# A hybrid decoder layer: projections by plain and by seven block products, block sums spread out, wider elementwise operations

## The chip, the cores and the metric

The kernel runs on one core of a Trainium2 chip. The metric is device time in microseconds (us). A core has a matrix engine (PE, with its weight loads listed apart as PEld), a vector engine (DVE), an activation engine (ACT), GpSimd (POOL) and a queue engine (SP) that issues most DMAs.

## What is computed

A decoder layer on x of 2048 tokens by 1024 features, all in float32. One projection feeds two mixers: a gated short convolution and a causal attention over three dilated windows. Their outputs are normalised, projected back, and a SwiGLU feed-forward follows.

```python
h = rms_norm(x, g_mix)
u, gb, gc, q, k, v = split(h @ w_in)          # six parts of 512 columns
y_conv = gb * short_conv(gc * u, conv_w)       # causal, width 3
q = rms_norm(q per head, g_q) * 64 ** -0.5     # 8 heads of 64
k = rms_norm(k per head, g_k)
y_attn = dilated_mixture(q, k, v)              # windows (128,1), (512,4), (2048,16)
x = x + concat(rms_norm(y_conv, g_conv_out), rms_norm(y_attn, g_attn_out)) @ w_out
h = rms_norm(x, g_ffn)
x = x + (silu(h @ w_gate) * (h @ w_up)) @ w_down
```

## The kernel before, in words

**Precision.** Each float32 operand is split into two float16 parts, hi and lo. A product is three float16 matmuls added up in PSUM (hi·hi, hi·lo, lo·hi). A split is a cast on ACT that gives hi, and a subtraction on another engine that gives lo.

**Tiles.** x is held as its transpose, in hi and lo, in four chunks c of 512 tokens; a chunk is eight tiles of 128 features by 512 tokens (`self.x[c]`). The 8 heads are taken as four pairs g.

**Stages.** The first is the norm of x with its DMA transposes, mixed with convolution block 0 (`conv_steps` with j = 0, called in `in_and_conv`): 4 chunks, and in each 3 products (gate C, u, gate B) of 24 matmuls. The second are the projections of q, k, v: 16 calls of `project(g, c, W)`, four chunks for each of four pairs; pair 3 takes the chunks backwards. The third is attention (`attention_pairs`, `attn_steps`): 160 steps, into which the rest of the convolution (blocks 1 to 3) and the half of the output projection that belongs to it (`tail_out`) are mixed as filler, `RATE` filler steps for each attention step. A filler step is three matmuls of 128x512 (`mm3_steps`, lines 191 to 193). The fourth are the other half of the output projection and the feed-forward; they aren't touched.

**Seven products of eight.** `project` multiplies a chunk of x (two token halves, two feature halves) by a pair's 384 columns (two column halves, one per head, of 192: q, k, v) by a scheme of seven block products in place of eight. It needs sums of blocks of both sides. `operands(g)` makes those of the weights: three loads, the largest element (`vmax`, a reduce of 3072 elements at L96), 8 scalings on ACT (L1163), combinations on GpSimd, and seven splits into tiles of the pool `ring` (ACT L1171, DVE L1172). `sums(c)` makes those of x, for two halves of a chunk: each takes two adds on GpSimd (L1134), four additions on DVE (L1137 to L1140), two casts on ACT (L1144) and two subtractions on DVE (L1145). Two `sums` calls stand in convolution block 0, two ahead of the first `project` calls.

**One call of `project`.** It works in two units t. A unit has three PSUM banks of 192 columns, from the pool `mm` or `cvx` in turn, and 84 matmuls (L1237). The banks are emptied into `f` while it runs: twice by ACT (L1247, L1254), five times by DVE (L1244). Then the epilogue: squares into `row` (ACT L1264), v split (ACT L1267, DVE L1268), sums of the squares (DVE L1274), a root by Ln and Exp (ACT L1275, L1276), and on GpSimd the scaling of q and k into `row` (L1285), the gain of k (L1290); then casts of `row` (ACT L1294, L1295) and subtractions (GpSimd L1296, L1297), and the stores to d_v and d_qk. There is one `row` and one `qkhl` for all calls.

**What else runs beside the projections.** `spill_conv(j, m)` splits the weights of convolution blocks 1 to 3, one third m at a time (through `weights`, ACT L149 and DVE L150, 8 of each) and writes them to DRAM for the filler. `spill_out` does so with the output weights (ACT L1333, DVE L1334). The table `SPILLS` says after which `project` call each runs.

**Order.** Each engine runs its instructions in the order in which they are written down; a scheduler that simulates the program sets that order. `tc.issue_after(x)` keeps what is emitted inside it from being placed before instruction x. Pools limit what is alive at once: `ring` has 9 tiles, `f` 3, `cvx` 4 PSUM banks.

Of the kernel before, what the change touches and what calls it, by code (L numbers as in the profile page):

```python
# [9 lines left out]
F32 = mybir.dt.float32  # L10
# [8 lines left out]
P = 128  # L19
# [7 lines left out]
HD = 64  # L27
# [983 lines left out]
class Fast(Builder):  # L1011
# [5 lines left out]
    RATE = 2.2  # L1017
# [16 lines left out]
    def in_and_conv(self):  # L1034
# [5 lines left out]
        with ExitStack() as c:  # L1040
# [11 lines left out]
            self.uc = cp.tile([P, 9], F32, name="uc")  # L1052
# [32 lines left out]
            ring = None  # L1085
            n = -1
            for step in self.conv_steps(0, W, before):
# [28 lines left out]
            self.st = dict()

    SPILLS = {(0, 3): (0,), (1, 0): (1, 2), (1, 2): (3,), (1, 3): (4,), (2, 0): (5, 6), (2, 2): (7,), (2, 3): (8,),
              (3, 0): (9, 10), (3, 1): (11, 12)}

    def sums(self, c, s0):
# [5 lines left out]
        Sc = self.sums_of[c] = [pool.tile([P, 2, 2, 4, 256], F16, name=name, bufs=2) for _ in range(2)]  # L1127
        xh, xl = self.x[c]
        for t in range(2):
            y = []  # L1130
            for i in range(2):
                o = slice((2 * t + i) * P, (2 * t + i + 1) * P)
                y.append(self.tmp.tile([P, KC, P], F32, name="t4"))
                nc.gpsimd.tensor_tensor(y[i], xh[:, :, o], xl[:, :, o], op=ALU.add)  # L1134
            a11, a12, a21, a22 = (y[i][:, 4 * k:4 * k + 4] for i in range(2) for k in range(2))
            v = nc.vector
            v.tensor_tensor(a22, a21, a22, op=ALU.add)  # L1137
            v.tensor_tensor(a21, a11, a21, op=ALU.subtract)
            v.tensor_tensor(a11, a22, a11, op=ALU.subtract)
            v.tensor_tensor(a12, a12, a11, op=ALU.subtract)  # L1140
            for i in range(2):
                src = y[i].rearrange("p (a k) t -> p a k t", a=2)
                hi, lo = (Sc[i][:, :, q, :, t * P:(t + 1) * P] for q in range(2))
                nc.scalar.copy(hi, src)  # L1144
                v.tensor_tensor(lo, src, hi, op=ALU.subtract)  # L1145

    def operands(self, g):
# [25 lines left out]
        p = nc.gpsimd  # L1173
        split(0, b11)
# [12 lines left out]
    def qk_constants(self):  # L1187
# [18 lines left out]
        self.vs = [self.fq.tile([P, 4, 2, 2, HD + 1], F16, name=f"vs{i}") for i in range(2)]  # L1206
# [4 lines left out]
    def project(self, g, c, W):  # L1211
# [8 lines left out]
        n = self.row.rearrange("p (j b d) -> p j b d", j=4, b=4)  # L1220
        F = []
        for t in range(2):
            pool, name = ((self.psmm, "mm"), (self.cvx, "cvx"))[self.units % 2]
            self.units += 1
            ps = [pool.tile([P, 512], F32, name=name)[:, 0:192] for _ in range(3)]

            def left(m, q, k):
                if m in (0, 1, 3):
                    i, k0 = {0: (2 * t, 0), 1: (2 * t, 4), 3: (2 * t + 1, 4)}[m]
                    return (xh, xl)[q][:, k0 + k, i * P:(i + 1) * P]  # L1230
                i, a = {5: (0, 0), 2: (0, 1), 6: (1, 0), 4: (1, 1)}[m]
                return Sc[i][:, a, q, k, t * P:(t + 1) * P]

            def product(m):
                for k in range(4):
                    for q, (x, y) in enumerate(((0, 0), (0, 1), (1, 0))):
                        nc.tensor.matmul(ps[self.BANK[m]], lhsT=left(m, x, k), rhs=W[m][:, y, k],  # L1237
                                         start=m in (0, 5, 4) and k == 0 and q == 0, stop=k == 3 and q == 2,
                                         skip_group_check=True)
            f = fq.tile([P, 2, 2, 192], F32, name="f", bufs=3)  # L1240
            F.append(f)

            def plus(o, bank, z):
                nc.vector.scalar_tensor_tensor(o, bank, u, z, op0=ALU.mult, op1=ALU.add)  # L1244
            f11, f12, f21, f22 = (f[:, i, h] for i in range(2) for h in range(2))
            product(0)
            nc.scalar.activation(f21, ps[0], AF.Copy, scale=u)  # L1247
            product(5)
            plus(f12, ps[1], f21)
            product(4)  # L1250
            if (g, c, t) == (0, 0, 0):
                self.squares(3, self.last, self.pstr.tile([P, 4], F32, name="tr"), False)
            product(1)
# [313 lines left out]
    def attention_pairs(self):  # L1567
# [9 lines left out]
        for _ in islice(fill, 24):  # L1577
            pass
# [315 lines left out]
```

## Time and profile before

| | us |
|---|---|
| median of 3 runs | 2207.26 (2206.59 to 2209.81) |
| the profiled execution | 2208.49 |
| its span in the trace | 2206.7 |
| PE busy | 2030.8 (92% of the span) |
| DVE busy | 1526.2 (69%) |
| ACT busy | 1047.4 (47%) |
| GpSimd busy | 726.7 (33%) |
| first matmul of the projections | at 132.71 |
| first matmul of attention (L1498) | at 473.35 |
| first matmul of the output projection's second half | at 836.92 |

Times in the trace count from the start of the span. A row of a window view gives busy time and number of instructions of each engine in a stretch, then PEclk (the clock that PE was granted, 1.00 is full), the mean busy share of the DMA engines, and GB/s. A row of the groups gives a line, its engine and operation, the tiles it writes and reads, a count, the busy time, the mean of one in ns, and the idle time ahead of them with what ended it. A row of the waits gives what was waited for, the total in us, how often, and the longest.

### The profile page before, as it was taken

To read this page: it belongs to the slowest core of one execution; us is meant where nothing else is said; L and a number is where in the kernel's file an instruction comes from. 1 tells how busy PE (TensorE), PEld (TensorE's weight loads), DVE (VectorE), ACT (ScalarE), POOL (GpSimd) and SP (SyncE) were. 2 spreads that over 40 slices of the span, in tenths; PEclk is the share of its full clock that TensorE was granted. 3 is DMA by queue.
4 is the path that set the end of the run, shared out by engine and by line. 5 is a ranking of instruction groups with operands and counts; after the bars stand their busy time and mean duration, and the time that the engine had idled before them with its cause. 6 is when DMAs were issued, how large, how long until landed. Compare 5 with 4: busy or idle time off the path is not lost.

```text
span 2206.7 us, 34303 instructions
## 1 busy us (share of the span) xinstructions
PE 2030.8 (92%) x12984; PEld 1115.8 (51%) x12984; DVE 1526.2 (69%) x2893; ACT 1047.4 (47%) x1967; POOL 726.7 (33%) x614
## 2 busy tenths in 40 slices
PE   3868778989999978998999999999999999999998
PEld 1347778946665653443444444444444444444443
DVE  7999885537776886687676666667676676545454
ACT  6445544447775766655333333334333244444341
POOL 2333434433433321122221112112222146555463
PEclk8879789999999998999999999999999999999999
DMA  9524454935867557799522332233222563251442
GB/s 240 138 84 138 158 154 130 192 74 148 180 136 193 167 140 200 244 248 293 161 101 91 101 115 82 91 107 113 90 95 102 210 243 123 77 178 53 130 139 87
DMA packets 460160, 317.00 MB, mean 144 GB/s; under 512 B 255568, under 2 KB 413264, under 8 KB 457808
## 3 DMA queue, kind: packets, MB, share of 16 engines
q1 hardware_dynamic: 442304, 291.56, 46.3%
q10 hardware_dynamic: 17680, 23.16, 2.9%
q8 instruction: 103, 1.69, 0.3%
q14 instruction: 73, 0.60, 0.1%
HBM read 157.96 MB, written 116.85 MB: 125 GB/s over the span
## 4 chain that ended last, share of the span: by engine, by line
PE 46%; issue 5%; DVE 4%; DMA 2%; SPq 2%; ACT 2%; POOL 1%; DVEq 0%; POOLq 0%; ACTq 0%
PE ps L812 28%; PE ps L945 15%; SPq L199 2%; DVE hl L680 1%; PE mm L191 1%; PE mm L192 1%; DVE w L933 1%; PE mm L193 1%; PE ps L191 1%; PE ps L192 0%; PE ps L193 0%; POOL x L952 0%; DMA b<-b 0%; ACT wq L742 0%; DMA wq<-d_a 0%
## 5 line engine op out<-in xcount | busy, mean ns | idle before, releaser
L812 PEld LDWEIGHTS <-w 128*128 128x128 f16 x3696 | 362.2, 98 | 448.0 <-issue 12.7
L812 PE MATMUL ps<-b,w 128*128 128x512 f16 x2112 | 464.8, 381 | 8.7 <-DMA b<-d_h 3.1
L945 PE MATMUL ps<-b,w 128*128 128x512 f16 x1848 | 399.7, 379 | 1.4 <-DVE s L966 0.8
L812 PE MATMUL ps<-hb,w 128*128 128x512 f16 x1584 | 347.1, 379 | 0.0
L945 PEld LDWEIGHTS <-w 128*128 128x128 f16 x1848 | 180.8, 98 | 220.1 <-issue 2.6
L705 POOL TENSOR_TENSOR t<-wq 128x512 f32<-128x512 f32 (+1 forms) x46 | 59.6, 1297 | 407.3 <-issue 231.1
L818 DVE TENSOR_TENSOR s<-ps,s 128x512 f32<-128x512 f32 x220 | 150.1, 683 | 37.1 <-PE ps L812 36.6
L952 POOL TENSOR_TENSOR x<-x,s 128x512 f32<-128x512 f32 x72 | 103.4, 1437 | 170.4 <-DVE s L966 133.1
L1511 DVE TENSOR_TENSOR et<-sm,et 128x512 f16<-128x512 f32 (+1 forms) x160 | 126.3, 807 | 41.8 <-ACT et L1510 40.8
L953 DVE SCALAR_TENSOR_TENSOR x<-ps,a_u,x 128x512 f32<-128x512 f32 x96 | 71.8, 749 | 101.7 <-PE ps L945 75.2
L1505 ACT ACTIVATE sm<-s,bound,kap 128x512 f32<-128x512 f32 (+1 forms) x160 | 116.6, 754 | 53.8 <-DVE s L1503 45.0
L191 PE MATMUL mm<-b,wq 128*128 128x512 f16 x320 | 125.7, 393 | 10.1 <-ACT cg L1360 8.6
L193 PE MATMUL mm<-b,wq 128*128 128x512 f16 x320 | 125.1, 391 | 3.4 <-DVE wq L150 3.4
L1237 PEld LDWEIGHTS <-b 128*128 128x128 f16 x1152 | 107.0, 105 | 40.1 <-issue 37.6
L192 PE MATMUL mm<-b,wq 128*128 128x512 f16 x320 | 125.1, 391 | 0.0
L722 ACT CAST w<-t 128x512 f16<-128x512 f32 x88 | 53.7, 616 | 129.2 <-PE ps L812 81.2
L1503 DVE TENSOR_TENSOR s<-s,mask 128x512 f32<-128x512 f32 (+1 forms) x128 | 80.0, 650 | 34.0 <-PE s L1498 33.6
L1516 PE MATMUL av<-v,et 128*128 128x65 f16 x1800 | 80.8, 195 | 18.2 <-DVE et L1511 16.2
L933 DVE TENSOR_TENSOR w<-t,w 128x512 f16<-128x512 f32 (+1 forms) x96 | 74.5, 794 | 32.9 <-ACT w L932 32.5
L846 ACT ACTIVATE sg<-s,w_un 128x512 f32<-128x512 f32 x66 | 47.3, 719 | 104.5 <-DVE s L818 104.5
L923 ACT ACTIVATE wq<-wq,asf 128x512 f32<-128x512 f32 x88 | 56.6, 711 | 81.5 <-DMA wq<-d_a 78.5
L932 ACT CAST w<-t 128x512 f16<-128x512 f32 (+1 forms) x96 | 53.4, 580 | 85.6 <-PE ps L945 59.8
(323 smaller groups left out, 3878.0 us busy)
## 6 DMA issues: line engine op xcount, KB each, us to landing
d_a<-a ACTq DMA_DIRECT2D x88, 256.0 KB, 2.0
d_wd<-w SPq DMA_DIRECT2D x77, 256.0 KB, 2.0
wq<-d_a SPq DMA_DIRECT2D x64, 256.0 KB, 4.0
b<-d_wd SPq DMA_DIRECT2D x14, 1024.0 KB, 5.7
d_qk<-qkhl SPq DMA_DIRECT2D x16, 768.0 KB, 4.0
d_h<-hl SPq DMA_DIRECT2D x24, 512.0 KB, 3.2
wq<-in_w_gate_dram SPq DMA_DIRECT2D x22, 512.0 KB, 4.7
wq<-in_w_up_dram SPq DMA_DIRECT2D x22, 512.0 KB, 5.0
```

The source lines that it names most:

```text
L191: self.pe = mm(ps, lhsT=lh(k), rhs=rh(k), start=k == ks[0], stop=False)
L192: mm(ps, lhsT=lh(k), rhs=rl(k), start=False, stop=False)
L193: mm(ps, lhsT=ll(k), rhs=rh(k), start=False, stop=k == ks[-1])
L812: nc.tensor.matmul(ps[self.BANK[n]], lhsT=w[:, x, k], rhs=b[:, y, k], start=first and k == 0 and q == 0, stop=k == 3 and q == 2, skip_grou ...
L818: nc.vector.tensor_tensor(t, x, y, op=ALU.add)
L933: nc.vector.tensor_tensor(L[n][:, 1, 0:n_f], src[n], L[n][:, 0, 0:n_f], op=ALU.subtract)
L945: nc.tensor.matmul(ps[self.BANK[n]], lhsT=L[n][:, x, f], rhs=B[n][:, f, y], start=first and f == 0 and q == 0, stop=f == n_f - 1 and q == ...
L952: nc.gpsimd.tensor_tensor(o, o, s_, op=ALU.add)
L1237: nc.tensor.matmul(ps[self.BANK[m]], lhsT=left(m, x, k), rhs=W[m][:, y, k], start=m in (0, 5, 4) and k == 0 and q == 0, stop=k == 3 and q ...
L1505: nc.scalar.activation(e, sp[:, 0:o], AF.Exp, scale=self.kap, bias=self.bound)
L1511: nc.vector.tensor_tensor(et[:, 1], e, et[:, 0], op=ALU.subtract)
L1516: self.pe_av = nc.tensor.matmul(av[:, us.index(u)], lhsT=p_, rhs=v_, start=n_ == 0, stop=n_ == len(ops) - 1)
```

## The change

1. `PLAIN = 2`: pairs 0 and 1 use plain products. `operands` makes four splits for them and no combinations. A call of `project` then has 4 blocks (token half i, column half h) of 48 matmuls, each in one bank of 384 columns from `cvx`, which ACT alone empties (after: L1264). That is 192 matmuls a call, where seven products take 168.
2. Pairs 2 and 3 keep the seven products, but a call is one unit with banks of 384 columns: the same 168 matmuls, and half as many operations to empty them, each twice as wide.
3. `sums(c, t)` makes one half of a chunk. The eight calls stand one ahead of each `project` of pairs 0 and 1; none is left in convolution block 0.
4. Sums, operands, gains and spills are emitted ahead of a `project` call, and after marks of the call before it: its v split on ACT and DVE, and the gain of k on GpSimd.
5. `spill_conv(j)` takes all three thirds at once: 8 scalings in place and three casts on ACT, three subtractions of 1024 elements on GpSimd; DVE has no part in the split any more. `spill_out` likewise: scaling in place and one cast on ACT, one subtraction on GpSimd, for each of two column halves; four calls.
6. The epilogue works on the whole call: one square of 1024 elements, one scaling on GpSimd of 1024. `f` has 2 buffers of a whole call, `ring` 8 tiles.
7. `q16` gets a pool of its own, opened ahead of attention's other pools; the first 24 filler steps are emitted after the last projection matmul; `RATE` is 1.95.

```diff
-    RATE = 2.2
+    RATE = 1.95
+    PLAIN = 2
...
-                    self.ring = e(tc.tile_pool(name="ring", bufs=9, side="right"))
+                    self.ring = e(tc.tile_pool(name="ring", bufs=8, side="right"))
...
-                elif n in (7, 9):
-                    self.sums(n // 2 - 3, s0)
+            self.marks = [self.dve.ins]
...
-                    if g == 0 and i < 2:
-                        self.sums(i + 2, s0)
-                    if g < 3 and i == 1:
-                        Wn = self.operands(g + 1)
+                    with ExitStack() as behind:
+                        for m in self.marks:
+                            behind.enter_context(tc.issue_after(m))
+                        if g < self.PLAIN:
+                            for _ in range(2 if self.PLAIN == 1 else 1):
+                                if wanted:
+                                    self.sums(*wanted.pop(0), s0)
+                        if g < 3 and i == 1:
+                            Wn = self.operands(g + 1)
...
+                        k = self.SPILLS.get((g, i))
+                        if k is not None:
+                            self.spill_conv(k) if k < 3 else self.spill_out((k - 3) // 2, (k - 3) % 2)
                     self.project(g, 3 - i if g == 3 else i, Wg)
...
+    SPILLS = {(0, 3): 0, (1, 2): 3, (1, 3): 1, (2, 0): 4, (2, 2): 5, (2, 3): 2, (3, 0): 6}
...
+        if g < self.PLAIN:
+            for n, x in ((0, b11), (1, b21), (2, b12), (3, b22)):
+                split(n, x)
+            return W
...
+        f = fq.tile([P, 2, 4, 192], F32, name="f", bufs=2)
...
+        if g < self.PLAIN:
+            for i in range(2):
+                for h in range(2):
+                    ps = self.cvx.tile([P, 512], F32, name="cvx")[:, 0:384]
+                    for k in range(2):
+                        product(ps, lambda t: x_(i, 4 * k, t), W[2 * h + k], k == 0, k == 1)
+                    nc.scalar.activation(block(i, h), ps, AF.Copy, scale=u)
...
+        for k in range(KC):
+            nc.scalar.activation(raw[:, k], raw[:, k], AF.Copy, scale=sg[:, k:k + 1])
+        for m in range(3):
+            w = self.tmp.tile([P, 2, KC, P], F16, name="t4")
+            src = raw[:, :, m * P:(m + 1) * P]
+            nc.scalar.copy(w[:, 0], src)
+            nc.gpsimd.tensor_tensor(w[:, 1], src, w[:, 0], op=ALU.subtract)
+            nc.sync.dma_start(self.d_wc[j][:, m], w)
...
+        with self.tc.issue_after(self.pe.ins):
+            for _ in islice(fill, 24):
+                pass
```

How the order changes, at two places. DVE, in convolution block 0, between the gate of one chunk (written to `cg`) and the `cu` of the next; `nx_` and L272 are the norm of x, whose results `ka` and `kb` the transposes read, `t_` and `s_` are tiles of `sums`. Before:

```order
L1379 SCALAR_TENSOR_TENSOR cg<-mm,w_un,cg 128x512
L74 SCALAR_TENSOR_TENSOR nx_y<-nx_t,nx_y 128x2
L1145 TENSOR_TENSOR s_840<-t_854,s_840 128x2x4x128
L1382 TENSOR_REDUCE yamax<-cg 128x1
L1137 TENSOR_TENSOR t_927<-t_927 128x512
L272 SCALAR_TENSOR_TENSOR ka<-nx_x,nx_y,ka 128x1024 x2
L1138 TENSOR_TENSOR t_927<-t_925,t_927 128x512
L272 SCALAR_TENSOR_TENSOR kb<-nx_x,nx_y,kb 128x1024 x2
L272 SCALAR_TENSOR_TENSOR ka<-nx_x,nx_y,ka 128x1024
L1139 TENSOR_TENSOR t_925<-t_927,t_925 128x512
L272 SCALAR_TENSOR_TENSOR ka<-nx_x,nx_y,ka 128x1024
L1373 SCALAR_TENSOR_TENSOR cu<-cvx,w_un,cg 128x512
```

After:

```order
L1415 SCALAR_TENSOR_TENSOR cg<-mm,w_un,cg 128x512
L272 SCALAR_TENSOR_TENSOR kb<-nx_x,nx_y,kb 128x1024
L1418 TENSOR_REDUCE yamax<-cg 128x1
L70 TENSOR_SCALAR nx_v<-nx_ss_663 128x2
L71 RECIPROCAL nx_y<-nx_y 128x2
L72 SCALAR_TENSOR_TENSOR nx_t<-nx_y 128x2
L73 TENSOR_TENSOR nx_t<-nx_t,nx_v 128x2
L74 SCALAR_TENSOR_TENSOR nx_y<-nx_t,nx_y 128x2
L272 SCALAR_TENSOR_TENSOR ka<-nx_x,nx_y,ka 128x1024 x2
L1409 SCALAR_TENSOR_TENSOR cu<-cvx,w_un,cg 128x512
```

The lines of `sums` (L1137 to L1145) are gone from between the norm's operations. The other place is GpSimd in the projections: one call's scaling (into `row`), gain, and subtractions (into `qkhl`). Before:

```order
L1285 TENSOR_TENSOR row<-f,qkr_y 128x512 x2
L1290 TENSOR_TENSOR row<-row,gk 128x8x64
L1310 COPY uc<-w_un 128x1
L1296 TENSOR_TENSOR qkhl<-row,qkhl 128x4x64 x2
L1297 TENSOR_TENSOR qkhl<-row,qkhl 128x4x64 x2
```

After, in pair 0 and 1 (L1142 are the adds of `sums`, L1344 the subtractions of `spill_conv`):

```order
L1142 TENSOR_TENSOR t_1811<-b_116,b_117 128x1024
L1142 TENSOR_TENSOR t_1813<-b_116,b_117 128x1024
L1321 TENSOR_TENSOR qkhl<-row,qkhl 128x4x64 x2
L1322 TENSOR_TENSOR qkhl<-row,qkhl 128x4x64 x2
L1344 TENSOR_TENSOR t_1857<-wq,t_1857 128x1024
L1344 TENSOR_TENSOR t_1861<-wq,t_1861 128x1024
L1312 TENSOR_TENSOR row<-f,qkr_y 128x1024
L1344 TENSOR_TENSOR t_1865<-wq,t_1865 128x1024
L1316 TENSOR_TENSOR row<-row,gk 128x8x64
```

Adds of `sums` now stand between the gain of one call and its subtractions, and a `spill_conv` puts two subtractions ahead of the next call's scaling and a third behind it.

More of the change, by code (lines that the diff above doesn't have):

```diff
@@ L1084, in in_and_conv @@
             self.sums_of = [None] * 4
-            ring = None
+            wanted = [(c, t) for c in range(4) for t in range(2)] if self.PLAIN < 4 else []
             n = -1
@@ L1128, in sums @@
         xh, xl = self.x[c]
[L1129 to L1145, printed above, removed]
+        y = []
@@ new lines, in sums @@
+        for i in range(2):
+            o = slice((t + 2 * i) * P, (t + 2 * i + 1) * P)
+            y.append(self.tmp.tile([P, KC, P], F32, name="t4"))
+            nc.gpsimd.tensor_tensor(y[i], xh[:, :, o], xl[:, :, o], op=ALU.add)
+        a11, a12, a21, a22 = (y[i][:, 4 * k:4 * k + 4] for i in range(2) for k in range(2))
+        v = nc.vector
+        v.tensor_tensor(a22, a21, a22, op=ALU.add)
+        v.tensor_tensor(a21, a11, a21, op=ALU.subtract)
+        v.tensor_tensor(a11, a22, a11, op=ALU.subtract)
@@ L1205, in qk_constants @@
         nc.gpsimd.memset(self.qkhl[:, :, 4:6, 1], 0.0)
[L1206 removed]
+        self.vs = [self.fq.tile([P, 2, 4, 2, HD + 1], F16, name=f"vs{i}") for i in range(2)]
         for t in self.vs:
@@ L1219, in project, with x_ @@
         vs = self.vs[c % 2]
-        n = self.row.rearrange("p (j b d) -> p j b d", j=4, b=4)
-        F = []
-        for t in range(2):
+        n = self.row.rearrange("p (h j b d) -> p h j b d", h=2, j=4, b=2)
+        f = fq.tile([P, 2, 4, 192], F32, name="f", bufs=2)
+        block = lambda i, h: f[:, h, 2 * i:2 * i + 2].rearrange("p t c -> p (t c)")
+        def x_(i, k0, t):
+            o = slice((t + 2 * i) * P, (t + 2 * i + 1) * P)
+            return lambda q, k: (xh, xl)[q][:, k0 + k, o]
@@ new lines, in s_, with product @@
+        def s_(i, a, t):
+            return lambda q, k: Sc[i][:, a, q, k, t * P:(t + 1) * P]
+        def product(ps, left, w, start, stop):
+            for t in range(2):
+                lh = left(t)
+                with self.tc.issue_after(first.ins) if t else nullcontext():
+                    for k in range(4):
+                        for q, (x, y) in enumerate(((0, 0), (0, 1), (1, 0))):
+                            self.pe = nc.tensor.matmul(ps[:, 192 * t:192 * (t + 1)], lhsT=lh(x, k), rhs=w[:, y, k],
+                                                       start=start and t + k + q == 0, stop=stop and k == 3 and q == 2,
+                                                       skip_group_check=True)
+                            if t + k + q == 0:
+                                first = self.pe
@@ new lines, in last_squares @@
+        def last_squares():
+            if (g, c) == (0, 0):
+                self.squares(3, self.last, self.pstr.tile([P, 4], F32, name="tr"), False)
+        if g < self.PLAIN:
+            for i in range(2):
+                for h in range(2):
[3 more added lines that the diff above has]
+                    nc.scalar.activation(block(i, h), ps, AF.Copy, scale=u)
+                last_squares() if i == 0 else None
+        else:
@@ L1234, in product @@
[L1234 to L1241, printed above, removed]
+            ps = [pool.tile([P, 512], F32, name=name)[:, 0:384] for _ in range(3)]
@@ L1243, in plus @@
+            f11, f12, f21, f22 = (block(i, h) for i in range(2) for h in range(2))
+            left = (lambda t: x_(0, 0, t), lambda t: x_(0, 4, t), lambda t: s_(0, 1, t), lambda t: x_(1, 4, t),
+                    lambda t: s_(1, 1, t), lambda t: s_(0, 0, t), lambda t: s_(1, 0, t))
             def plus(o, bank, z):
                 nc.vector.scalar_tensor_tensor(o, bank, u, z, op0=ALU.mult, op1=ALU.add)
-            f11, f12, f21, f22 = (f[:, i, h] for i in range(2) for h in range(2))
-            product(0)
@@ L1247, in project @@
[L1247 to L1253, printed above, removed]
-            nc.scalar.activation(f11, ps[0], AF.Copy, scale=u)
-            product(6)
-            plus(f22, ps[1], f21)
-            plus(f22, ps[2], f22)
-            product(3)
-            plus(f21, ps[1], f21)
```

114 lines of the change are left out of this document (63 added, 51 removed).

## The prediction

> **What bounds the kernel now.** I read the page first, for the clock slices, and then a table of windows cut at the stages' borders, since a share over the whole span hides where PE waits.
>
> ```profile
> span 2206.7 us, 34303 instructions
> PEclk8879789999999998999999999999999999999999
> DMA  9524454935867557799522332233222563251442
> ```
>
> A slice is 55 us. PE's clock is under 0.9 in slices 1 to 3, 5 and 6 (0 to 331 us) and once more in 16 (827 to 883): the time is lost early, and the DMA engines are full there only in slice 1.
>
> ```profile
> core 0: us, PE busy (x) PEld busy (x) DVE busy (x) ACT busy (x) POOL busy (x), PEclk, DMA share, GB/s
> 25.00:127.00 102.00, 77.04 (x341) 36.74 (x342) 96.02 (x139) 50.80 (x80) 36.57 (x15) 0.86 0.61 153
> 127.00:155.00 28.00, 10.92 (x80) 9.27 (x80) 26.72 (x55) 16.14 (x28) 13.22 (x11) 0.66 0.20 60
> 155.00:451.30 296.30, 251.20 (x2659) 238.17 (x2660) 216.22 (x569) 145.30 (x345) 117.64 (x125) 0.91 0.59 155
> 451.30:473.40 22.10, 13.48 (x53) 5.50 (x51) 5.17 (x10) 5.04 (x12) 14.29 (x16) 0.77 0.28 87
> 473.40:824.00 350.60, 327.35 (x3640) 216.31 (x3638) 265.58 (x459) 248.07 (x474) 115.24 (x92) 0.97 0.61 151
> 837.00:2206.70 1369.70, 1350.73 (x6216) 609.76 (x6216) 893.61 (x1548) 558.93 (x987) 424.69 (x333) 0.99 0.44 139
> 404.00:437.00 33.00, 33.00 (x403) 33.00 (x401) 17.43 (x46) 15.09 (x35) 12.29 (x16) 1.00 1.09 194
> ```
>
> From 837 on PE is busy 99% at full clock, and nothing there is edited. Attention (473 to 824) has PE at 93%. What can be won lies ahead of 473: in the norm and convolution block 0 (25 to 127) DVE is busy 96 of 102 us and PE 77; then 28 us (127 to 155) in which PE does 80 of the projections' matmuls, at clock 0.66, with DVE at 95%; then the projections, PE at 85% and clock 0.91. The last row is a stretch in the projections without a wait: 33.00 us for 403 matmuls, 81.9 ns each. That is my price of a projection matmul.
>
> Then PE's waits, the first two rows from 25 to 127, the others from 127 to 452, and the timeline at the borders (PE, and SP's queue).
>
> ```profile
> PE cvx L191 <- DMA b<-kb: 11.5, 2, 8.2
> PE mm L193 <- DVE wq L150: 3.4, 1, 3.4
> ```
>
> ```profile
> PE cvx L1237 <- ACT f L1247: 19.7, 9, 4.7
> PE mm L1237 <- DVE f L1244: 15.1, 8, 4.1
> PE mm L1237 <- ACT w L1171: 11.9, 3, 6.7
> PE cvx L1237 <- DVE f L1244: 9.6, 6, 2.8
> ```
>
> ```profile
> 96.37 5.30 SPq L199 DMA_TRANSPOSE b<-kb  x4
> 101.72 1.20 SPq L1154 DMA_DIRECT2D wq<-in_w_in_dram  x2
> ```
>
> ```profile
> 100.53 1.03 PE L191 MATMUL cvx<-b,wq 128*128 128x512 f16 x2 [8.24 <-DMA b<-kb]
> 132.71 0.32 PE L1237 MATMUL mm<-w,b 128*128 128x192 f16 x1 [4.92 <-ACT w L1171]
> 465.54 0.58 PE L191 MATMUL mm<-b,wq 128*128 128x512 f16 x1 [8.62 <-ACT cg L1360]
> 470.55 0.38 PE L191 MATMUL mm<-b,wq 128*128 128x512 f16 x1
> 473.14 0.38 PE L191 MATMUL mm<-b,wq 128*128 128x512 f16 x1
> 473.35 0.27 PE L1498 MATMUL s<-q,ka 128*128 128x256 f16 x1
> ```
>
> In block 0 PE waits for the transposes of the last chunks (8.24 us before 100.53), and these for DVE's norm. In the projections it waits for banks to be emptied, by ACT and by DVE, and at the change of pairs for a weight split (L1171). ACT's emptying is itself late behind the epilogue, below. From 470.55 to 473.14 PE issues 12 filler matmuls, 216 ns each.
>
> **The change part by part.** All times are against the profiled execution, 2208.49 us (span 2206.7 and 1.8 around it); the median is 1.2 below it.
>
> *(a) Block 0 without sums.* On tiles `t`, which here are those of the sums alone:
>
> ```profile
> 45.00:97.00 52.00, 23.62 (x22) 6.06 (x6) 19.11 (x8) 0.92 0.54 137
> ```
>
> DVE gets 23.6 of these 52 us back. Not all reaches the transposes, since the DMAs have loads of x to bring. PE's two waits above, 11.5 + 3.4, bound the gain at 15 us; the lower end is 4 (DVE filling its gaps with other norm work at no gain for the last chunk). I take 12, near the upper end, as DVE is at 94% and the norm stands behind the sums in its order. The last transposes then end at 89.7 in place of 101.7.
>
> *(b) The first operands.* From the loads (101.72) to the first projection matmul (132.71) it is 31.0 us. The work in it:
>
> ```profile
> L96 DVE TENSOR_REDUCE vm_a<-wq 128x1 f32<-128x3072 f32 x3 | 10.0, 3349 | 0.0
> L1163 ACT ACTIVATE wq<-wq,w_sg 128x384 f32<-128x384 f32 x32 | 16.8, 602 | 4.4 <-DVE w_sg L1161 4.4
> L1171 ACT CAST w<-wq 128x768 f16<-128x768 f32 x28 | 22.5, 826 | 11.6 <-PE cvx L1237 11.6
> L1134 POOL TENSOR_TENSOR t<-b,b 128x1024 f32<-128x1024 f16 x16 | 39.6, 2485 | 88.3 <-DMA b<-ka 30.6 <-DVE qT L1145 18.7 <-DVE ka L1145 17.1
> ```
>
> 3.35 + 8 x 0.60 + 0.83 is 9.0; issue, landing, the small steps of the maximum and the lo part I put at 12 (an estimate: what is left of the 31 after DVE's queue, which is full of sums there). So 21, between 16 and 31, and the projections begin near 89.7 + 21 = 111, where they now begin at 133; range 105 to 121. They then have all weights as DVE splits them, four in place of seven, and no sums ahead: the starved stretch 127 to 155, in which 28 us do 80 x 0.082 = 6.6 us of work, goes with it.
>
> *(c) The projections.* Pairs 0 and 1 have 192 matmuls a call and pairs 2 and 3 168: 8 x 360 = 2880, where 16 x 168 = 2688 stood. At 81.9 ns that is 235.9 us, 15.7 more than before. To it comes what PE loses, X. Before, in 155 to 451, 2612 product matmuls are recorded:
>
> ```profile
> 155.00:451.30 296.30, 241.60 (x2612) 233.56 (x2612) 0.91 0.59 155
> ```
>
> 296.3 - 2612 x 0.0819 - (2659 - 2612) x 0.216 = 72 us lost, 27.6 ns for each. Some 45 of it is idle (296.3 - 251.2), the rest half clock after it. What sets it now is the loop through the one `row`:
>
> ```profile
> L1264 ACT ACTIVATE row<-f 128x512 f32<-128x512 f32 x32 | 19.9, 626 | 38.0 <-DVE f L1244 26.0 <-POOL qkhl L1297 7.4 <-DVE w_m L81 4.2
> L1274 DVE TENSOR_REDUCE qk_ss<-row 128x16 f32<-128x1024 f32 x16 | 19.4, 1212 | 1.3 <-ACT row L1264 1.3
> L1285 POOL TENSOR_TENSOR row<-f,qkr_y 128x512 f32<-128x512 f32 x30 | 32.5, 1105 | 97.0 <-DVE qkr_y L1280 96.3 <-DVE w_sg L147 0.7
> L1290 POOL TENSOR_TENSOR row<-row,gk 128x512 f32<-128x512 f32 x15 | 19.3, 1285 | 1.1
> L1296 POOL TENSOR_TENSOR qkhl<-row,qkhl 128x256 f16<-128x256 f32 x30 | 21.3, 731 | 3.6 <-ACT qkhl L1294 3.6
> L1247 ACT ACTIVATE f<-cvx,uq 128x192 f32<-128x192 f32 x16 | 6.7, 417 | 30.3 <-POOL row L1285 30.3
> ```
>
> The last row shows it: ACT's first emptying idles 30.3 us for GpSimd's scaling, which still reads `f`. The loop's work is 2 x 0.63 + 1.21 + 2 x 1.11 + 1.29 + 4 x 0.73 = 8.9, with some 3 us for the small steps and casts (estimate) 12 us a call. PE takes 192 x 0.082 = 15.7 or 168 x 0.082 = 13.8 a call, so the loop fits by itself; what comes between on the same queues decides. In pairs 0 and 1 that is two adds of 2.49 on GpSimd, put right inside it: 17 against 15.7. A plain call waits for nothing but ACT's copies, one per 48 matmuls (3.9 us), each between 0.42 (192 wide) and 0.63 (the 512-wide square), with four banks. I give these eight calls 10 us (0 to 25). In pairs 2 and 3 half of the 72 would stay if nothing else changed; half as many emptyings, and no `spill` work on DVE, make it less, but at two changes of pairs the splits still wait for `ring`, now of 8, and the old waits there come to 11.9. I give 32 (20 to 47). X is 42, between 20 and 72.
>
> *(d) Moved work.* GpSimd gets 17 subtractions of 1024 (nine in `spill_conv`, eight in `spill_out`). No subtraction of that width is in this trace; as four of 256 (0.73) each costs 2.9, by the add of 1024 it costs 2.49. I take 2.5, as the shape is that of the add: 42 us, hidden as GpSimd is free for 60% of 155 to 451 (117.6 of 296.3), but without that cover it would be 42 on the path. GpSimd's sum over the projections: 16 x 2.49 + 32 x 1.11 + 16 x 1.29 + 64 x 0.73 + 42 = 185 us of 278. A rule of the Trainium skill ("GPSIMD Engine Reference", section 4.1) speaks against this: an elementwise operation of two inputs is to go to VectorE, being about twice as slow on GpSimd. By it, with DVE's time for the same split
>
> ```profile
> L150 DVE SCALAR_TENSOR_TENSOR t<-t,w_sg,t 128x128 f16<-128x128 f32 x72 | 25.7, 408 | 1.2 <-ACT t L149 1.0
> ```
>
> doubled, 17 subtractions would be estimated at 17 x 2 x 8 x 0.41 = 111 us in place of 42, and GpSimd would have 254 us in 278: it would then be the bound (R2). No run here shows that price yet, and the add's row is nearer in shape.
>
> *(e) Ahead of attention.* By the order, 96 filler matmuls stand between the last product and the first S: 96 x 0.216 = 20.7. The wait of 8.62 at 465.54, and clock 0.77 around it, go, since the filler's weights are written by then. S begins at 111 + 235.9 + 42 + 20.7 = 410, where it began at 473.4: 63.7 us earlier.
>
> *(f) Attention.* The same work; 24 + 20 filler steps stand elsewhere. Of 356 filler steps 332 are left after the first 24: at 2.2 a step they end by step 151 of 160, and the last nine have no cover; at 1.95 they last 160 steps, with 20 left over. I give it 3 us, of the 23 that PE idles there (350.6 - 327.4), bounds 8 slower to 8 faster. The epilogue's wider operations do the same elements in fewer instructions; I put them at nothing (two squares of 0.63 bound one of 1024), hidden by ACT's and GpSimd's idle half of the projections; without that cover they are in the loop's 12 us.
>
> Sum: 2208.5 - 63.7 - 3 = 2141.8; less the 1.2 between profile and median, 2141 us.
>
> A second rule of the skill bears on X ("TensorE: Matmul & The Clock Gate", section "What's actually happening"): the clock halves after an idle window of about 3.4 us and takes as long to come back. If plain calls had only short waits, X would be estimated at the idle alone, 45/72 of 42, 26 us, and the time at 2125, inside my case. Against it stands that before the waits averaged 19.7/9 = 2.2 us and the clock was 0.91 all the same; I keep 42.
>
> **The rivals.**
>
> *R1: the loss per matmul stays.* The epilogue, not the emptying, sets PE's pace, and the loop is unchanged in kind. Then X is 2880 x 27.6 ns = 79: 37 above mine, 2178. For it: L1247 waits for GpSimd, and GpSimd gets more. Against it: plain calls need DVE for no bank.
>
> *R2: GpSimd's queue becomes the bound, slower.* Adds of the sums (5.0) and spill subtractions (7.5 with three) stand in the loop: 12 + 5 + 7.5 = 24.5 where both fall in one call, against 15.7. No gain is left when the mean call reaches (473.4 - 20.7 - 111)/16 = 21.4 us; at 23 the time is 2207 + 16 x 1.6 = 2233. For it: GpSimd's mean call is 185/16 = 11.6 at my price, but 254/16 = 15.9, already PE's own pace, if a subtraction costs twice DVE's 3.3. Against it: only one call in four has spills, and two `f` let PE run ahead one call.
>
> *R3: attention gives part back.* The 20 steps left over run alone at the end, 60 x 0.216 = 13 us, and 3 are not won: with the rest as I have it, 2141 + 13 = 2154. The order has filler between the last attention matmuls, which speaks against.
>
> *R4: no change.* The projections start earlier, but waits eat it: PE loses 106 us in place of 42, 2205. That is 27 us over R1's 79, for which no row speaks. That sums stay in block 0 is excluded by the order.
>
> **How the numbers follow.** My case 0.60, R3 0.12, R1 0.18, R4 0.03, R2 0.07. The likeliest is 2141. Low end: start at 105 (6), X of 20 (22) and attention 8 (5) hardly come together; most of that is 2110. High end: R1 with a start some 6 later, 2185. Left out are R2, R4 and the tails. About 0.2% (4.4 us) is what a measurement can tell from no change. Faster 0.90, same 0.03, slower 0.07.
>
> **What would show it.** In the profile after: the first projection matmul near 111; the projections some 278 us long with PE clock over 0.93; S near 410; waits on L1264 small in pairs 0 and 1; the output projection's second half near 770; GpSimd's subtraction near 2.5. I am wrong if S begins after 430, or if a wait for GpSimd (f, row) leads PE's list.

## The result and the profile after

The changed kernel takes 2171.96 us (median of 4 runs, 2170.41 to 2176.61) beside 2208.14 for the kernel before: ratio 0.984, interval 0.9821 to 0.9858. It is 1.6% faster, and inside the range, but by 36 us, where 67 were forecast; 2172 lies nearer to rival R1 (2178) than to 2141.

First the page of the changed kernel.

```profile
span 2168.7 us, 34196 instructions
PEclk9999899999999999999999999999999999999999
```

The slices with a low clock are gone but for one, the fifth. Then the windows at the new borders: two stretches of the plain pairs, two of the others, the filler behind them, attention, and all from the output projection's second half on.

```profile
core 0: us, PE busy (x) PEld busy (x) DVE busy (x) ACT busy (x) POOL busy (x), PEclk, DMA share, GB/s
103.30:170.00 66.70, 65.95 (x796) 65.80 (x796) 49.38 (x89) 34.91 (x60) 26.54 (x24) 1.00 0.43 112
170.00:241.70 71.70, 64.02 (x752) 63.28 (x750) 54.42 (x59) 40.71 (x70) 56.96 (x34) 0.95 0.37 97
241.70:323.00 81.30, 59.02 (x674) 57.16 (x672) 65.49 (x112) 46.08 (x76) 47.78 (x36) 0.94 0.52 145
323.00:405.10 82.10, 61.57 (x672) 59.14 (x672) 49.26 (x94) 40.91 (x77) 47.03 (x35) 0.92 0.92 212
405.10:429.70 24.60, 20.91 (x99) 9.41 (x97) 10.33 (x15) 10.23 (x20) 12.14 (x12) 1.00 1.08 220
429.70:779.90 350.20, 324.28 (x3640) 213.84 (x3639) 270.32 (x476) 247.13 (x476) 131.25 (x102) 0.98 0.64 158
786.60:2168.70 1382.10, 1352.93 (x6216) 609.41 (x6216) 891.56 (x1551) 559.05 (x988) 423.93 (x333) 0.99 0.45 138
```

The first stretch (pair 0 and a little of pair 1) runs at full clock with 0.75 us idle, the second with 7.7; pairs 2 and 3 have 672 matmuls each, 55.0 us of work at 81.9 ns, and take 81 and 82. Last, the timeline at the borders (SP's queue, then PE).

```profile
78.57 5.40 SPq L199 DMA_TRANSPOSE b<-kb  x4
84.03 2.23 SPq L1162 DMA_DIRECT2D wq<-in_w_in_dram  x3
```

```profile
103.27 0.24 PE L1249 MATMUL cvx<-w,b 128*128 128x192 f16 x1 [0.36 <-ACT w L1179]
429.73 0.37 PE L1534 MATMUL s<-q,ka 128*128 128x256 f16 x1 [3.71 <-DVE qkr_t L1308]
786.62 0.60 PE L191 MATMUL mm<-b,b 128*128 128x512 f16 x1 [6.85 <-ACT b L585]
```

| us from the span's start | before | forecast | after |
|---|---|---|---|
| first projection matmul | 132.7 | 111 | 103.3 |
| projections end | 451.3 | 389 | 405.1 |
| first S of attention | 473.4 | 410 | 429.7 |
| output projection's second half | 836.9 | 770 | 786.6 |
| end of the span | 2206.7 | 2140 | 2168.7 |

Against the forecast the end comes 29 us late. The start is 8 us better, the projections 24 worse (302 us, where 278 were forecast), the filler behind them 4 worse, attention with the idle stretch behind it 3 better, and the last stage 12 worse (1382 us; 1370 before and in the forecast). PE's waits in the projections of the changed kernel, the largest first:

```profile
PE mm L1249 <- ACT f L1279: 11.2, 2, 10.4
PE mm L1249 <- DVE f L1275: 10.5, 6, 3.3
PE mm L1249 <- ACT w L1179: 9.0, 3, 7.8
PE cvx L1249 <- ACT f L1264: 7.7, 3, 5.5
PE cvx L1249 <- DVE f L1275: 6.8, 5, 1.9
```

L1279 and L1275 empty the banks of the seven products, L1264 those of the plain ones, L1179 splits weights. Only the fourth row is of a plain pair. No row names GpSimd, so the list alone doesn't say why ACT and DVE were late.

### The profile page after: what moved, and what is told of

It reads as the page before. It is cut to its first block, busy times and chain, and to the rows that moved or that the text cites. A ratio compares the mean times of both kernels' runs of the same rounds, so it can differ in the third digit from the quotient of the medians.

```text
span 2168.7 us, 34196 instructions
## 1 busy us (share of the span) xinstructions
PE 2016.9 (93%) x13176; PEld 1111.9 (51%) x13176; DVE 1457.2 (67%) x2581; ACT 1043.0 (48%) x1882; POOL 756.7 (35%) x598
## 4 chain that ended last, share of the span: by engine, by line
PE 57%; DVE 16%; DMA 8%; ACT 6%; issue 5%; POOL 3%; SPq 3%; DVEq 0%; ACTq 0%; POOLq 0%
PE ps L812 27%; PE ps L945 18%; SPq L199 2%; PE mm L192 2%; PE mm L191 2%; DVE et L1547 2%; PE mm L193 2%; PE s L1534 2%; DVE vm_a L96 1%; ACT sm L1541 1%; PE av L1552 1%; DMA wq<-in_w_up_dram 1%; DMA wq<-in_w_gate_dram 1%; DMA t<-in_w_out_dram 1%; DVE w L723 1%
## 5 line engine op out<-in xcount | busy, mean ns | idle before, releaser
L812 PEld LDWEIGHTS <-w 128*128 128x128 f16 x3696 | 362.3, 98 | 454.5 <-issue 17.2
L812 PE MATMUL ps<-b,w 128*128 128x512 f16 x2112 | 467.4, 382 | 12.7 <-DMA b<-d_h 5.1
L812 PE MATMUL ps<-hb,w 128*128 128x512 f16 x1584 | 347.1, 379 | 0.0
L1249 PEld LDWEIGHTS <-b 128*128 128x128 f16 x2112 | 180.5, 100 | 39.9 <-issue 38.3
L1249 PE MATMUL cvx<-w,b 128*128 128x192 f16 x1824 | 156.6, 249 | 16.2 <-ACT f L1264 7.7
L952 POOL TENSOR_TENSOR x<-x,s 128x512 f32<-128x512 f32 x72 | 103.1, 1433 | 171.1 <-DVE s L966 132.7
L1547 DVE TENSOR_TENSOR et<-sm,et 128x512 f16<-128x512 f32 (+1 forms) x160 | 133.9, 854 | 37.1 <-ACT et L1546 36.2
L192 PE MATMUL mm<-b,wq 128*128 128x512 f16 x320 | 122.1, 382 | 0.0
L191 PE MATMUL mm<-b,wq 128*128 128x512 f16 x320 | 122.1, 382 | 0.0
L193 PE MATMUL mm<-b,wq 128*128 128x512 f16 x320 | 122.1, 381 | 0.0
L96 DVE TENSOR_REDUCE vm_a<-wq 128x1 f32<-128x2048 f32 (+2 forms) x32 | 77.3, 2416 | 52.9 <-DMA wq<-in_w_up_dram 25.0
```

The costliest lines, as they stand in the source:

```text
L96: e.tensor_reduce(a[:, i:i + 1], x, axis=AX.X, op=ALU.max, apply_absolute_value=True)
L191: self.pe = mm(ps, lhsT=lh(k), rhs=rh(k), start=k == ks[0], stop=False)
L192: mm(ps, lhsT=lh(k), rhs=rl(k), start=False, stop=False)
L193: mm(ps, lhsT=ll(k), rhs=rh(k), start=False, stop=k == ks[-1])
L812: nc.tensor.matmul(ps[self.BANK[n]], lhsT=w[:, x, k], rhs=b[:, y, k], start=first and k == 0 and q == 0, stop=k == 3 and q == 2, skip_grou ...
L952: nc.gpsimd.tensor_tensor(o, o, s_, op=ALU.add)
```

## The experiments

Three theories; C was added when the first four runs (all plain, all plain with two rows, the mark, spills on DVE) were known. A: the loop through the one `row` (square, sums of squares, root, scaling, gain, casts, subtractions, the next square) sets the pace. B: seven products cost their own waits, for emptied banks and splits. C: the sums of x, made beside the plain pairs, cost PE time there or later.

**All pairs plain.** `PLAIN = 4`: no sums and no combinations are left.

```diff
-    PLAIN = 2
+    PLAIN = 4
```

> All four pairs by plain products (16 x 192 x 0.0819 = 251.6 us of product matmuls, 15.7 more than the changed kernel); no sums and no combinations are left. Theory A, the loop through the one row (square, reduce, root, scaling, gain, casts, subtractions, next square; 20.2 us a call in the changed kernel) sets the pace: with the 16 pairs of adds and the seven combinations gone from GpSimd and DVE the loop falls to about 17 us a call, the projections from 302 to about 272 us, the time to about 2145. Theory B, PE's own waits for emptied banks and split weights set the pace, each for itself: the DVE waits (17 us) and half of the waits for splits (12) go, 15.7 us of matmuls come, so 2160 to 2165.

Measured 2119.12 us, ratio to before 0.9601 (0.9581 to 0.962): 53 us faster than the changed kernel, and better than either theory said. The projections:

```profile
103.30:370.50 267.20, 257.67 (x3080) 256.48 (x3080) 125.00 (x259) 152.75 (x279) 126.86 (x114) 0.99 0.72 177
```

3072 x 0.0819 = 251.6 us of 267.2 are matmuls: 15.6 lost, where the changed kernel loses 301.8 - 235.9 = 66. The 15.7 us more of matmuls are paid back three times. B as I priced it fails, as its forecast was 2160 or more; A's 272 us for the projections is near, but the next runs give A no support.

**All plain, and two rows.** All pairs plain again, with two rows and two `qkhl` in turn.

```diff
-        n = self.row.rearrange(
+        self.calls += 1
+        n = (self.row, self.row2)[self.calls % 2].rearrange(
...
-        hl = self.qkhl
+        hl = self.hls[self.calls % 2]
```

> As the run with four plain pairs, with two rows and two qkhl used in turn, so that a call's square no longer waits for the subtractions of the call before. Theory A: PE's matmuls become the bound, 252 us and about 10 of losses, 262 us for the projections and about 2135. Theory B: the row was no bound, so as the run with four plain pairs, within 3 us.

2125.38 us, 0.9626 (0.961 to 0.9642): no faster than with one row. With all pairs plain, the row isn't what binds; it says nothing yet of the changed kernel, where the loop is slower. The starts of the squares, first and last of 16, in the changed kernel, with all plain, and in the next run of this kind:

```profile
L1294 ACT ACTIVATE row<-f x16: 1042/1057/1061, 122.0 to 424.8; 128x1024 f32<-128x1024 f32 x16
```

```profile
L1294 ACT ACTIVATE row<-f x16: 1041/1057/1058, 121.9 to 378.3; 128x1024 f32<-128x1024 f32 x16
```

```profile
L1296 ACT ACTIVATE row<-f x16: 1047/1057/1059, 122.2 to 412.8; 128x1024 f32<-128x1024 f32 x16
```

One call takes (424.8 - 122.0)/15 = 20.2 us, 17.1 with all plain.

**Two rows in the changed kernel.** To make room, `ring` has 7 tiles and there is one `vs`; `qkhl` stays one.

```diff
-bufs=8, side="right"))
+bufs=7, side="right"))
...
-        n = self.row.rearrange(
+        n = (self.row, self.row2)[self.calls % 2].rearrange(
```

> The changed kernel (two plain pairs, two of seven products) with two rows used in turn; to make room the ring has 7 tiles in place of 8 and there is one vs in place of two. Theory A: squares no longer wait for the subtractions of the call before (19.8 us of ACT's idle time in the changed kernel), the call falls from 20 to about 17 us: 2140 to 2150. Theory B or C: 2170 to 2178, the smaller ring making it a little slower.

2180.04 us, 0.9883 (0.9856 to 0.9909): 8 more than the changed kernel, and the intervals just touch. The call shortens only to 19.4 us, and PE waits longer for splits:

```profile
PE mm L1251 <- ACT w L1180: 15.6, 4, 8.6
```

That was 9.0 with a ring of 8. So nothing speaks for A: a second row alone doesn't free PE. The run doesn't refute A either, as what the smaller ring and the single `vs` took back isn't told apart.

**The mark moved.** GpSimd's mark goes from the gain to the last subtraction, to keep other work from between them.

```diff
-        self.marks.append(p.tensor_tensor(nk, nk, ..., op=ALU.mult).ins)
+        p.tensor_tensor(nk, nk, ..., op=ALU.mult)
...
-            p.tensor_tensor(hl[:, :, 4 + h, 0], k, hl[:, :, 2 + h, 0], op=ALU.subtract)
+            last = p.tensor_tensor(hl[:, :, 4 + h, 0], k, hl[:, :, 2 + h, 0], op=ALU.subtract)
+        self.marks.append(last.ins)
```

> Only the mark on GpSimd moves, from the gain of k to the last subtraction: adds of the sums, combinations and subtractions of the spills can no longer stand between the gain and the subtractions of a call. Theory A: two adds (4.6 us) leave the loop in eight calls, some of it comes back as later scaling; 10 to 20 us less, about 2157. Theory B: no gain, 0 to 5 us slower, since sums and operands come later: 2172 to 2177.

2177.14 us, 0.9853 (0.9833 to 0.9872): no gain, if anything 5 slower. In the changed kernel's trace adds stand between the gain and the last subtraction in six calls, here in none; a spill's subtraction stands there in four. So taking the adds out of that place gains nothing; that they are there at all may still cost.

**Spills' subtractions back on DVE**, with two plain pairs and with four.

```diff
-            nc.gpsimd.tensor_tensor(w[:, 1], src, w[:, 0], op=ALU.subtract)
+            nc.vector.tensor_tensor(w[:, 1], src, w[:, 0], op=ALU.subtract)
...
-            nc.gpsimd.tensor_tensor(w[:, 1], raw, w[:, 0], op=ALU.subtract)
+            nc.vector.tensor_tensor(w[:, 1], raw, w[:, 0], op=ALU.subtract)
```

> The 17 subtractions of the spills go back from GpSimd to DVE, the rest stays. Theory A: neither engine is full (GpSimd 59%, DVE 72% of the projections), the subtractions stand in the loop on either; within 5 us of 2172. The rival that GpSimd's subtractions are the cost (17 x 2.3 = 39 us on its queue): 15 us or more less, 2157 or below.

2168.09 us, 0.9814 (0.9798 to 0.983), 4 less than the changed kernel, with intervals that overlap.

> Four plain pairs, and the 17 subtractions of the spills back on DVE, which without the sums is busy 125 of 267 us there. GpSimd (127 of 267) gets as much relief as DVE gets load: 2114 to 2122, no difference if PE's matmuls are the bound of the projections (252 of 267).

2124.55 us, 0.9615 (0.9588 to 0.9642), 5 more than all plain with GpSimd, and within what can be told apart. The same subtraction, on GpSimd in the changed kernel and on DVE in the run with two plain pairs:

```profile
L1344 POOL TENSOR_TENSOR t<-wq,t 128x1024 f16<-128x1024 f32 x9 | 20.9, 2323 | 8.1 <-ACT t L1343 5.2 <-issue 2.9
```

```profile
L1344 DVE TENSOR_TENSOR t<-wq,t 128x1024 f16<-128x1024 f32 x9 | 12.0, 1347 | 5.7 <-ACT t L1343 5.6
```

2.32 against 1.35 us: GpSimd takes 1.7 times as long, and it costs 4 us or nothing. This edit isn't where the gain went.

**Three pairs plain.** One pair by seven products, sums for it all the same.

```diff
-    PLAIN = 2
+    PLAIN = 3
```

> Pairs 0 to 2 plain, only pair 3 by seven products. Sums of x are still made, all eight. Theory B (each pair of seven products costs its own waits, for emptied banks and for its splits): half of the 53 us that four plain pairs gained, about 2145. Theory C (the sums' work on DVE and GpSimd beside the plain pairs is the cost): most of it stays, 2155 to 2165.

2155.59 us, 0.9769 (0.9744 to 0.9794). Turning pair 2 plain gains 16 us, pair 3 another 36: with the last pair go the sums. That speaks for C, and the next run divides the 36.

**All plain, with the sums made for nobody.**

```diff
-            wanted = [(c, t) for c in range(4) for t in range(2)] if self.PLAIN < 4 else []
+            wanted = [(c, t) for c in range(4) for t in range(2)]
...
-                        if g < self.PLAIN:
+                        if g < 2:
```

> Four plain pairs, but the eight calls of sums are made all the same, beside pairs 0 and 1, and nobody uses them. Theory C: 20 us or more of the 53 are lost again, 2140 to 2150. Theory B: nothing waits for them, at most the 10 us that the changed kernel lost in pairs 0 and 1: 2119 to 2129. Theory A (the loop through the one row): the adds lengthen it from 17 to 20 us in eight calls, 24 us less what the two buffers of f hide: 2130 to 2143.

2154.15 us, 0.9757 (0.9733 to 0.9782): 35 of the 53 us are lost again, by work whose results no one reads. C holds. With the sums made, it matters little whether pair 3 is plain: 2154 here, 2156 in the run before. The projections, and PE's waits, first from 103 to 250, then from 250 to 425:

```profile
103.30:396.10 292.80, 265.43 (x3084) 262.48 (x3083) 173.21 (x293) 162.93 (x285) 161.71 (x118) 0.95 0.65 158
```

```profile
PE cvx L1249 <- ACT f L1264: 5.5, 1, 5.5
```

```profile
PE cvx L1249 <- ACT w L1179: 10.8, 1, 10.8
PE cvx L1249 <- ACT f L1264: 9.1, 4, 3.4
PE s L1534 <- POOL q L1445: 6.6, 1, 6.6
```

The sums add 48 us to DVE and 35 to GpSimd. They aren't over by 250: the last two adds run at 279.5 to 283.7, the last subtraction ends at 294.3 (in the changed kernel 283.7 and 295.1, inside pair 2). Beside all plain, this run is 8 us behind when pair 1 ends (240.1 against 231.7), 14 to 22 behind around the end of the sums, 25.7 at the end of the projections, and 34.5 at the first S (419.3 against 384.8). So about half of the loss shows while the sums are made, the rest later.

The trace shows how it builds up. The epilogue falls behind first: the square of a call starts 1.0, 5.9, 7.2, 10.5, 16.7 and 21.5 us after the call's last product in the first six calls, and 1.0, 5.9, 7.2, 10.5, 16.7 and 20.0 in the changed kernel; with all plain and no sums it is never over 5.1. In calls 2 to 6 PE loses 0.1 us each all the same. In the seventh call it loses 8.0 (7.5 in the changed kernel). DVE, then ACT, in this run ahead of that wait:

```profile
197.01 3.34 DVE L96 TENSOR_REDUCE vm_a<-wq 128x1 f32<-128x3072 f32 x1
207.13 2.71 DVE L1153 TENSOR_TENSOR ka<-t,ka 128x1024 f16<-128x1024 f32 x1
209.76 1.23 DVE L1169 TENSOR_SCALAR w_sg<-gin_g,w_s 128x8 f32<-128x8 f32 x1
```

```profile
211.03 0.61 ACT L1171 ACTIVATE wq<-wq,w_sg 128x384 f32<-128x384 f32 x1 [3.04 <-DVE w_sg L1169]
212.15 3.65 ACT L1171 ACTIVATE wq<-wq,w_sg 128x384 f32<-128x384 f32 x7
217.47 0.57 ACT L1264 ACTIVATE f<-cvx,uq 128x384 f32<-128x384 f32 x1
```

The scale `w_sg` of pair 2's weights stands behind five operations of the sums on DVE (L1145 to L1148 and L1153, 5.8 us): from the reduce at 197.01 to `w_sg` it takes 12.8 us, 6.9 with all plain. ACT waits for it, scales, and only then empties the bank (217.47) that PE has waited 5.52 us for. The run below with GpSimd's part alone loses 0.1 us in the seventh call, the one with DVE's part 6.6.

Over the whole stage ACT's square waits for GpSimd's subtractions, first in the changed kernel, then here; with all plain this wait comes to 4.3 us.

```profile
ACT row L1294 <- POOL qkhl L1322: 19.2, 10, 4.8
```

```profile
ACT row L1294 <- POOL qkhl L1322: 20.2, 11, 5.0
```

**Only GpSimd's part of the sums, and only the part of DVE and ACT.** Both are edits of the last run. In the first, `sums` returns after the adds. In the second, ACT copies the hi part of x in place of the adds, so that GpSimd has no part (the sums' values are wrong there; nothing reads them).

```diff
+        return
         a11, a12, a21, a22 = (y[i][:, 4 * k:4 * k + 4] for i in range(2) for k in range(2))
```

> Four plain pairs; of the unused sums only the two adds on GpSimd are made in each of the eight calls (16 x 2.3 = 37 us of GpSimd), nothing of their DVE and ACT part, and their tiles stay empty. If GpSimd's adds, which stand in front of a call's subtractions, are the larger part of the 35 us that making all of the sums cost: 2138 to 2150. If it is DVE's part: 2119 to 2126.

```diff
-            nc.gpsimd.tensor_tensor(y[i], xh[:, :, o], xl[:, :, o], op=ALU.add)
+            nc.scalar.copy(y[i], xh[:, :, o])
```

> Four plain pairs; the unused sums are made with their DVE and ACT part, but ACT copies (1.04 us each) take the place of the adds on GpSimd; the sums' values are wrong, and unused. If DVE's part (some 50 us of its queue in eight calls) is the cost: 2145 to 2155, as with all of the sums. If it takes both engines at once (DVE's operations of two inputs grow longer beside GpSimd's): 2125 to 2140.

2137.06 us, 0.9666 (0.9639 to 0.9692), and 2143.91 us, 0.97 (0.9673 to 0.9727): 18 and 25 us above all plain, 35 with both. Their projections, in this order:

```profile
103.30:382.90 279.60, 259.81 (x3083) 257.83 (x3082) 124.47 (x258) 150.97 (x276) 151.94 (x120) 0.98 0.69 171
```

```profile
103.30:390.50 287.20, 262.90 (x3084) 260.33 (x3083) 168.55 (x305) 179.10 (x308) 134.72 (x107) 0.96 0.66 167
```

Each part costs by itself; neither engine alone is the cause. 25 us more on GpSimd, then busy 54% of the stage, cost 12 us in the projections; 44 more on DVE and 26 on ACT, at 59% and 62%, cost 20. Of the 26, some 17 are the 16 copies that stand for the adds, which the sums don't have, so the 25 us of time aren't all DVE's part.

**The kernel before, with its sums ahead of the calls of pair 0.**

```diff
-                elif n in (7, 9):
-                    self.sums(n // 2 - 3, s0)
...
-                    if g == 0 and i < 2:
-                        self.sums(i + 2, s0)
+                    if g == 0:
+                        self.sums(i, s0)
```

> The kernel before, with one edit of the change: no sums in convolution block 0; each call of pair 0 makes those of its own chunk ahead of itself. Block 0 should end about 13 us earlier, as it did in the changed kernel. But the first seven products of a chunk then wait for its sums, 13 us of DVE a chunk, in four calls: if the plain pairs are what makes the move pay, 2195 to 2215, about no change; if the block's relief is all, 2180.

2206.66 us, 1.0 (0.9987 to 1.0013). It doesn't test what it was made for: on the tiles `t` the trace has

```profile
45.00:97.00 52.00, 23.47 (x23) 6.06 (x6) 19.11 (x8) 0.93 0.56 139
```

the sums' work where it was. Nothing held it back, and the scheduler placed it in block 0 again. So no run shows the move out of block 0 by itself. In the changed kernel that window has none of it, as the sums stand behind marks. Even there two adds, those of the first call, run in block 0, at 25.87 and 34.56: a mark sets the place in the order, and GpSimd had nothing else ahead of them (its last operation started at 4.07). So block 0 isn't quite free of sums, though I had written that none is left there.

**The rate of the filler.** `RATE` back to 2.2 in the changed kernel.

```diff
-    RATE = 1.95
+    RATE = 2.2
```

> The changed kernel with 2.2 filler steps for each attention step, as in the kernel before. If the slower rate gains what the prediction put down for attention: 2175 to 2180. If what it fills ahead of the output projection is given back behind it (6.7 us won there, 10 us lost by the feed-forward's start): within 3 us of 2172.

2180.03 us, 0.986 (0.9831 to 0.9889): the slower rate gains 8 us by the medians, 4 by the ratios, and the intervals overlap. In the two traces 8.7 of 9.0 us lie between the first S and the output projection's second half (365.6 us here, 356.9 in the changed kernel).

## Why the prediction was right, and where it fell short

The direction and the range were right; the gain was about half of the forecast, since the projections (c) lost more than the sum allowed, and the last stage, which had no term, lost 12. S behind 430 was to show me wrong. It began at 429.7, and that is luck: a start 8 us better than forecast made up for a part of (c).

**(a) Block 0: right, too small.** The transposes end at 84.0, 17.7 us earlier (12 forecast), past my upper bound of 15. That bound counted only PE's two waits. The stretch up to the end of the transposes, before and after:

```profile
25.00:101.70 76.70, 57.13 (x259) 27.42 (x259) 73.94 (x107) 43.97 (x71) 26.75 (x11) 0.87 0.66 161
```

```profile
25.00:84.00 59.00, 51.34 (x257) 25.97 (x256) 37.08 (x77) 34.48 (x62) 4.38 (x2) 1.00 0.97 206
```

PE idles 11.9 us less, inside the bound, and is busy 5.8 us less for nearly the same matmuls, at clock 1.00 in place of 0.87: that part had no term.

**(b) The first operands: right.** From the loads at 84.03 to the first projection matmul it takes 19.2 us, where I put 21 out of bounds of 16 and 31. The start is 29 us earlier.

**(c) The projections: here the sum failed.** X was to be 42, and is 66, near R1's 79. What PE loses in each pair, counted from call to call in the traces as time less 81.9 ns for each product matmul and 216 ns for each of the filler:

| us lost in pair | 0 | 1 | 2 | 3 |
|---|---|---|---|---|
| before | 33.2 | 33.0 | 21.0 | 1.1 |
| changed | 2.2 | 10.3 | 26.6 | 26.9 |
| all plain | 2.2 | 0.4 | 9.1 | 3.9 |
| all plain, sums for nobody | 1.8 | 8.3 | 25.8 | 4.4 |

The plain pairs are near the forecast: 12.5 us where I put 10, of which 7.5 is the seventh call. Pairs 2 and 3 lose 53.5 where I put 32. The step that failed is the one that halved the 72 for these pairs and took some off for relieved engines. Before, the loss wasn't spread evenly: pairs 2 and 3 had only 22 of it, so that the change more than doubled theirs. I had priced the sums only as two adds on GpSimd in pairs 0 and 1 (within the 10), put nothing for their work on DVE, and called the spills hidden because GpSimd had idle time.

The runs show that the moved sums cost 35 us in a kernel that doesn't need them, with the engines 55 to 60% busy, and that the largest part of this falls in pair 2: 25.8 us there with the sums and no seven products, 9.1 without the sums, 26.6 in the changed kernel. Pair 3 is another matter: 4.4 us with the sums alone, 26.9 in the changed kernel. Seven products as such don't have to cost that, as pair 3 lost 1.1 with them before. Then the scale `w_sg` of its weights was ready 137 us ahead of the pair (247.9, pair at 385.0); in the changed kernel, where operands stand behind marks, it comes 9.5 us ahead (313.7, pair at 323.2), and PE waits 9.0 us for the splits. Whether the marks, the wide calls, the smaller ring or the moved spills do this was not tried. What remains of the 53 us to all plain, 18, goes with these and with the combinations, seven splits in place of four and the emptying by DVE, less the 15.7 us of matmuls that seven products save. That my loop through `row` (12 us a call, measured 20.2) is the way the price is paid is not shown: a second row didn't help, moving the adds out of it didn't, and the ring of 7 blurs the first of these.

I had also worked out 26 for X, without slower clock. Of the 66, 51 are idle (301.8 - 250.6) and 15 slower clock, so both parts were larger than that.

**(d) GpSimd's subtractions: right.** 2.32 us where I put 2.5, and hidden but for at most 4, which the intervals don't tell from nothing. The Trainium skill ("GPSIMD Engine Reference", section 4.1) has two-input operations about twice as slow there as on VectorE; the trace shows 1.7 (2.32 against 1.35). I had doubled the wrong row: DVE's own time for this shape is 1.35, not 8 x 0.41, so R2's 254 us were never near.

**(e) Ahead of attention:** 24.6 us where I put 20.7; the rest is the wait of 3.71, put down to the last call's root (L1308).

**(f) Attention: right; behind it a loss without a term.** Attention takes 350.2 us as before (350.6), but the idle stretch ahead of the output projection falls from 13.0 to 6.85, so 6.6 us are gained from the first S on, where I put 3. The last stage, for which I put nothing as nothing there is edited, gives that back and more. PE's waits there, before and after:

```profile
PE ps L812 <- DMA b<-d_h: 3.1, 1, 3.1
PE ps L812 <- ACT s L863: 2.9, 1, 2.9
PE mm L191 <- DVE qT L599: 2.4, 1, 2.4
```

```profile
PE mm L191 <- DVE qT L599: 6.4, 1, 6.4
PE ps L812 <- DMA b<-d_h: 5.1, 3, 2.2
PE ps L812 <- ACT s L863: 4.9, 1, 4.9
```

PE waits for the half of the output projection that DVE evacuates (L599) and for loads and activations of the feed-forward: 8 us more. That PE comes sooner isn't the reason: with all plain it comes another 51 us sooner, and from the first matmul of L812 to the end it takes 1225.3 us, 1226.4 in the changed kernel and 1217.7 before. The rate isn't it either, as the last stage takes 1381.9 us with `RATE` at 2.2. The cause stays open.

**The rivals.** R1's time was nearly right (2178); its even loss per matmul wasn't: 27.6 ns forecast, 8 in the plain pairs and 40 in the others. Its reason, that the epilogue keeps PE's pace, is half right: the epilogue lags, and more so beside the sums. R2 and R3 didn't come: PE's list names GpSimd nowhere, GpSimd is busy 178 of 302 us, and behind attention there are 6216 matmuls as before, so no filler is left over. With all plain 42 filler matmuls are (9 us), and hardly a gap stands ahead of the output projection.

## What to carry to other kernels

Work moved beside a full engine isn't free because the engine that takes it is half idle. It stands in the in-order queues that feed the full engine; here PE lost 0.1 us a call while the epilogue fell 20 us behind, and the bill came in the next pair and the next stage. Price it by making that work for nobody in a version that doesn't need it; here the price (35 us) was over twice what the seven products saved (15.7), and the plainest version, 2119 us, beat both kernels. Moving code moves instructions only if something holds them: check in the trace where they stand.

## What the runs showed of the hardware

A DVE operation on 16 columns can last until GpSimd's operation beside it ends. DVE (root of the squares) and GpSimd in the changed kernel, start and length:

```profile
328.53 2.09 DVE L1307 TENSOR_SCALAR qk_ss<-qk_ss 128x16 f32<-128x16 f32 x1
330.53 0.16 DVE L1308 SCALAR_TENSOR_TENSOR qkr_t<-qkr_y 128x16 f32<-128x16 f32 x1
330.73 1.66 DVE L1309 TENSOR_TENSOR qkr_t<-qkr_t,qk_ss 128x16 f32<-128x16 f32 x1
```

```profile
327.92 2.66 POOL L1370 TENSOR_TENSOR t<-t,t 128x1024 f16<-128x1024 f32 x1
330.55 1.81 POOL L1189 TENSOR_TENSOR wq<-wq 128x768 f32<-128x768 f32 x1
```

```profile
L1307 DVE TENSOR_SCALAR qk_ss<-qk_ss x16: 159/167/2099, 128.2 to 427.6; 128x16 f32<-128x16 f32 x16
```

L1307, 0.167 us at the median, ends at 330.62 with GpSimd's operation (330.58); L1309 ends at 332.39 with the next one (332.36). The Trainium skill ("SBUF — State Buffer", section "Who interferes with whom") says that the two share a port pair and that, where they contend for it, one holds it for a whole instruction; the trace agrees. Of the 16 executions of L1307, eleven have no GpSimd operation beside them and take 0.159 to 0.175 us; five have one, take 0.58 to 2.10 us, and each ends within 0.05 us of a GpSimd operation's end. So GpSimd's long operations lengthen the short steps of DVE's chain, by up to 1.9 us each, and the busy share counts the waiting as work.
